# Inner norms: the summands of the tokens' tiles are added by adding transfers from memory, VectorE only multiplies

## The chip, the cores and the metric

The kernel runs on one core of one Trainium2 chip. The metric is the device time of one execution in microseconds; it is 1188.16 us before the change (median of 3 runs, 1187.76 to 1188.19). TensorE, VectorE, ScalarE, GpSimd and SyncE are called PE, DVE, ACT, POOL and SP, as in the profile.

## The reference, cut to what matters

Two layers, each of three post-norm steps on 256 tokens of width 1024, in float32:

```
for l in range(2):
    h = (silu(x @ w1) * (x @ w3)) @ w2            # width 2816
    x = LN(ALPHA * x + 0.5 * h) * g[l, 0] + b[l, 0]
    h = mixer(x)                                  # gated unit and differential attention
    x = LN(ALPHA * x + h) * g[l, 1] + b[l, 1]
    h = (silu(x @ w1') * (x @ w3')) @ w2'
    x = LN(ALPHA * x + 0.5 * h) * g[l, 2] + b[l, 2]
```

`g` and `b` are rows of 1024 numbers, the same for all tokens. The norm of the last step writes the output. The other five are the inner norms: their x is the input of the next step's products and also the term ALPHA * x of the next norm. The mixer's attention turns q and k by rotary angles: each pair of rows is multiplied by a cosine, the pair with its rows exchanged by a sine, and the two are added.

## The kernel before, in words

**Products.** The weights stream from memory once, in pieces of 128x2048 floats (1 MB), each fetched by SP into one of 4 buffers `raw`. ACT rounds a half of a piece to a high part (`whi`, L195 or L247), DVE subtracts it to get the low part (`wlo`, L197 or L249), and PE multiplies x, itself in a high and a low part, with both. The order of PE's instructions is written out by hand. On the other engines a scheduler sets the order when the kernel is built, by a priority that grows with every fetch, by expected times, and by some orders that the code asks for (`behind`, L158). It follows that an instruction taken away can move others on its engine. Within an engine the order is then fixed, and an instruction whose inputs are late holds all that follow it there. Results leave PE through 4 main banks of PSUM in rotation and 4 side banks.

**The inner norms** (class `Norm`). The tokens lie in two tiles `x_tok[0]` and `x_tok[1]` (`xtok` in the profile, 128 tokens by 1024 floats each). When a step ends, DVE adds the new term to these tiles (`part`, `fold`), takes mean and variance, and normalises them in place (`finish`). Then two things happen. The normalised tiles are turned to columns, scaled and shifted there by ACT (`affine`), and split for the next step's products: PE needs these at once. And the tiles themselves are multiplied by g and increased by b (`tokens`, L703), because the next norm, 100 us or more later, starts from them. For that, `bc_load` (L585) has POOL load g and b, each spread over 128 partitions, into two buffers with the tag `bc` (512 KB each); a one-column copy by DVE (L587) sets the earliest moment of the load. The two `bc` buffers also hold two tiles `planes` of the feed-forward step in turn, and the mixer's rows `gbias`, `g_bc` and `b_bc`.

**POOL's queue.** POOL issues the transfers that go through the software queue: the loads by `bc_load` and the adding transfers of `gather` (L353). These add 512 KB of weights from memory to a buffer in place, with `accum_op=ALU.add`; there are 22 of them before the change. Between them POOL copies the halves of 32-bit numbers apart and together for transposing transfers (L216, L229, L741), and multiplies in the mixer (L977).

**The mixer's first part.** After the columns of v, four pairs of calls of `rope` (L968), q and k of two heads each. A call streams 1 MB of weights through PE (16 matmuls of 512 columns with the high part and 16 of 256 with the low, 5.6 us), and its result comes out in two halves from two banks: ACT copies one part (`r`, L303), DVE adds the other (`z`, L305 or L307). Then SP issues two transfers that exchange neighbouring rows of z into `swap` (L973), DVE multiplies z by the cosine (L976), POOL multiplies `swap` by the sine (L977), and DVE adds both (L981). After each pair of calls `attend` (L987) follows in steps put beside later products: PE takes the scores (L1001), DVE and ACT the softmax (L1013, L1015), DVE the difference `d` of the two maps (L1024), POOL parts it for a transposing transfer of SP's queue (L216, L220), ACT joins it (L1049), and PE multiplies it with v (L1055, L1057).

In the list of functions, L numbers are those of the profile.

Of the kernel before, what the change touches and what calls it, by code (L numbers as in the profile page):

```python
# [17 lines left out]
ALU = mybir.AluOpType  # L18
AX = mybir.AxisListType

P = 128
# [33 lines left out]
def trunk(ctx, tc, x, xT, w13a, w13b, w2, wb, wqk, wu, wg, wgr, wbr, wbrr, wo, gateb, gatebr, sgug, sgub, sguwT, sgubias, lam, diffg,  # L55
          lng, lnb, lngT, lnbT, cosT, sinT, out):
    nc = tc.nc
    V, A, G, PE = nc.vector, nc.scalar, nc.gpsimd, nc.tensor
# [15 lines left out]
    def name(s):  # L74
        serial[0] += 1
        return f"{s}_{serial[0]}"
# [24 lines left out]
    def s512(s, n=4):  # L101
        return tmp.tile([P, 512], F32, tag="side", name=name(s), bufs=n)

    def sm(s, n, dtype=F32, bufs=2):
        return small.tile([P, n], dtype, tag=f"{s}{n}", name=name(s), bufs=bufs)
# [31 lines left out]
    def beside(task, delay):  # L137
        tasks.append([clock[0] + delay, task])
# [16 lines left out]
    def behind(ins):  # L155

        return tc.issue_after(ins) if ins is not None else nullcontext()
# [427 lines left out]
    def bc_load(src, after):  # L585
        t = res.tile([P, D], F32, tag="bc", name=name("bc"), bufs=2)
        V.tensor_copy(t[:, :1], after)  # L587
        spread[0] = G.dma_start(t, src.partition_broadcast(P)).ins
        return t

    class Norm:
# [6 lines left out]
        def __init__(self, l, i, scale, eps, after, last=False):  # L598
            self.scale, self.eps, self.last, self.done, self.front = scale, eps, last, set(), i
            self.ends, self.xhi, self.xlo, self.rows = [None] * NT, {}, {}, {}  # L600
            self.gT, self.bT = (v[:, l, i] for v in (ln_g, ln_b))
            self.y = x_tok
            self.group = 256 if last else 512
            self.st = [sm("st", D // self.group * 6, bufs=2) for _ in range(NT)]
            self.g, self.b = bc_load(lng[l, i], after), bc_load(lnb[l, i], after)
            if last:
                beside(self.halved(), 9)
                self.minus = s512("minus")
                A.activation(self.minus[:, :P], ident, AF.Copy, scale=-1.0)
                self.eps_t = self.minus[:, 2 * P : 2 * P + 1]  # L610
                V.memset(self.eps_t, eps)
                with behind(silu[0]):
                    A.activation(sm("first", 1), mask[:, :1], AF.Sqrt)
            else:
                self.via = []
                self.x = [xs.tile([P, 4, 512], F32R, tag="x", name=name("x")) for _ in range(2)]
# [85 lines left out]

        def tokens(self, t):  # L703
            with behind(added[0] if self.front else self.xlo[1, 1]):
                for v, op in ((self.g, ALU.mult), (self.b, ALU.add)):
                    V.tensor_tensor(out=self.y[t], in0=self.y[t], in1=v, op=op)
            yield 0

        def sent(self):
# [632 lines left out]
```

## Time and profile before

| what | value |
|---|---|
| time, median of 3 runs | 1188.16 us (1187.76 to 1188.19) |
| time of the profiled execution | 1187.27 us |
| its span in the profile | 1185.6 us, so 1.7 us lie around it |
| PE busy | 1180.0 us, 5775 matmuls |
| DVE busy | 1013.4 us (85%) |
| ACT, POOL busy | 826.7 us (70%), 281.7 us (24%) |
| PE clock granted | 1.0 throughout |
| bytes moved | 275.10 MB, 232 GB/s on average |

All times of single instructions are those of the one profiled execution, counted from the start of its span. An instruction that runs back to back with the next is shown with a little overlap (a DVE operation of 1.22 us is followed after 1.14). A row of the timeline has the start, the duration, engine, line, operation, output and inputs, and in brackets how long the engine stood idle before it and who ended that. A row of the windows has, after each engine's busy time, the granted clock, the share of the 16 DMA engines that was busy, and GB/s. The transfer groups show the median time from issue to landing.

### The profile page before, as it was taken

The numbers are of one execution on the slowest core, as the hardware profiler recorded it, in microseconds if no ns is written. First come the engines' busy times: TensorE is split into PE (matmuls) and PEld (weight loads), VectorE is DVE, ScalarE is ACT, GpSimd is POOL, SyncE is SP. The second block draws the span as 40 slices with busy tenths as digits, with TensorE's granted clock in tenths as the row PEclk, the third lists the DMA queues.
The fourth block names the chain that finished last, engine by engine and source line by source line (L and its number), as shares of the span: only waits on it lengthen the run. The fifth ranks groups of instructions, "written<-read, shape, count | busy, mean of one in ns | idle before, by whom it ended". The sixth has DMA issues, their size and how long they took to land.

```text
span 1185.6 us, 16672 instructions
## 1 busy us (share of the span) xinstructions
PE 1180.0 (100%) x5775; PEld 994.6 (84%) x5775; DVE 1013.4 (85%) x1560; ACT 826.7 (70%) x1417; POOL 281.7 (24%) x352
## 2 busy tenths in 40 slices
PE   9999999999999999999999999999999999999998
PEld 8888888888888888888888888888888888888887
DVE  7989989788688989889898889888965989988895
ACT  6688658559855677876667876676788556679761
POOL 1012201247420220061020141004564112102300
PEclk9999999999999999999999999999999999999999
DMA  9868976758865658689668689586666755786881
GB/s 358 262 199 260 289 274 210 263 191 239 245 211 169 224 194 271 188 272 272 232 223 264 194 278 271 200 300 224 216 203 203 257 182 165 260 247 210 272 253 36
DMA packets 129620, 275.10 MB, mean 232 GB/s; under 512 B 89040, under 2 KB 90368, under 8 KB 105472
## 3 DMA queue, kind: packets, MB, share of 16 engines
q1 hardware_dynamic: 121968, 248.67, 63.4%
q0 software_dynamic: 6992, 24.71, 8.9%
q8 instruction: 45, 0.74, 0.2%
q10 hardware_dynamic: 576, 0.66, 0.2%
q14 instruction: 39, 0.32, 0.1%
HBM read 248.05 MB, written 1.05 MB: 210 GB/s over the span
## 4 chain that ended last, share of the span: by engine, by line
PE 99%; DVE 0%; DVEq 0%; issue 0%
PE bank L283 46%; PE bank L295 15%; PE sbank L376 12%; PE bank L410 10%; PE bank L302 8%; PE sbank L410 3%; PE bank L527 2%; PE sbank L1001 1%; PE bank L376 1%; PE sbank L1057 1%; PE sbank L1175 1%; PE sbank L539 0%; PE sbank L1055 0%; PE sbank L698 0%; DVE xtok L685 0%; DVE xtok L679 0%
## 5 line engine op out<-in xcount | busy, mean ns | idle before, releaser
L197 DVE TENSOR_TENSOR wlo<-raw,whi 128x1024 fp32r<-128x1024 f32 (+1 forms) x346 | 378.3, 1121 | 53.0 <-ACT whi L195 39.7
L195 ACT ACTIVATE whi<-raw 128x1024 fp32r<-128x1024 f32 (+1 forms) x350 | 323.0, 951 | 131.7 <-PE bank L283 43.0
L283 PE MATMUL bank<-whi,x 128*128 128x512 f32 x1224 | 386.3, 390 | 0.0
L283 PEld LDWEIGHTS bank<-whi,x 128*128 128x128 f32 x1224 | 229.8, 188 | 47.6
L283 PE MATMUL bank<-wlo,x 128*128 128x512 f32 x612 | 238.2, 389 | 0.0
L249 DVE TENSOR_TENSOR wlo<-raw,whi 128x1024 fp32r<-128x1024 f32 (+1 forms) x123 | 143.8, 1193 | 21.4 <-ACT whi L247 12.5
L247 ACT ACTIVATE whi<-raw 128x1024 fp32r<-128x1024 f32 (+1 forms) x123 | 121.1, 1003 | 52.4 <-DVE raw L359 18.2
L295 PE MATMUL bank<-x,whi 128*128 128x512 f32 x640 | 153.3, 391 | 0.0
L295 PEld LDWEIGHTS bank<-x,whi 128*128 128x128 f32 x640 | 118.2, 188 | 23.8
L283 PEld LDWEIGHTS bank<-wlo,x 128*128 128x128 f32 x612 | 114.9, 188 | 23.4
L302 PEld LDWEIGHTS bank<-x,wlo 128*128 128x128 f32 x640 | 81.4, 191 | 2.9
L229 POOL COPY seven<-seven 128x512 uint16<-128x512 uint16 x16 | 49.4, 3130 | 140.4 <-ACT whi L195 54.6
L302 PE MATMUL bank<-x,wlo 128*128 128x256 f32 x640 | 82.6, 283 | 0.0
L410 PE MATMUL bank<-whi,hhi 128*128 128x512 f32 (+1 forms) x182 | 68.2, 374 | 0.0
L410 PE MATMUL bank<-whi,hlo 128*128 128x512 f32 (+1 forms) x182 | 67.9, 373 | 0.0
L410 PE MATMUL bank<-wlo,hhi 128*128 128x512 f32 (+1 forms) x182 | 67.9, 373 | 0.0
L977 POOL TENSOR_TENSOR swap<-swap,sin_t 128x512 f32<-128x512 f32 x16 | 27.8, 1735 | 101.8 <-DMA swap<-z 52.2
L741 POOL COPY nvia<-ntwo 128x256 uint16<-128x256 uint16 x20 | 9.9, 543 | 162.0 <-DMA ntwo<-nvia 142.5
L303 ACT ACTIVATE r<-bank 128x256 f32<-128x256 f32 x96 | 34.8, 372 | 16.7 <-PE bank L302 16.5
L376 PE MATMUL sbank<-whi,xhs 128*128 128x512 f32 x128 | 42.0, 389 | 0.0
L410 PEld LDWEIGHTS bank<-whi,hlo 128*128 128x128 f32 x182 | 34.3, 188 | 6.1
L410 PEld LDWEIGHTS bank<-wlo,hhi 128*128 128x128 f32 x182 | 34.3, 188 | 5.9
(285 smaller groups left out, 2158.7 us busy)
## 6 DMA issues: line engine op xcount, KB each, us to landing
raw<-in_w13b SPq DMA_DIRECT2D x68, 1024.0 KB, 6.1
raw<-in_w SPq DMA_DIRECT2D x32, 1024.0 KB, 7.0
raw<-in_wb SPq DMA_DIRECT2D x16, 1024.0 KB, 6.1
raw<-in_wqk SPq DMA_DIRECT2D x16, 1024.0 KB, 6.1
home<-in_w13b SPq DMA_DIRECT2D x16, 512.0 KB, 6.0
raw<-in_w13a SPq DMA_DIRECT2D x8, 1024.0 KB, 5.0
home<-in_w SPq DMA_DIRECT2D x16, 512.0 KB, 4.0
raw<-in_wgr SPq DMA_DIRECT2D x8, 1024.0 KB, 5.3
```

The costliest lines, as they stand in the source:

```text
L195: inline(A, A.activation(h, r, AF.Copy).ins)
L197: low = eng.tensor_tensor(out=w, in0=r, in1=h.bitcast(F32), op=ALU.subtract).ins
L229: eng.tensor_copy(out=o, in_=i)
L247: a = A.activation(hi, src, AF.Copy).ins
L249: return a, eng.tensor_tensor(out=lo, in0=src, in1=hi.bitcast(F32), op=ALU.subtract).ins
L283: PE.matmul(ps, xx, w, start=start and n == 0, stop=stop and n == 2)
L295: PE.matmul(b[-1], hi[:, k * P : (k + 1) * P], xc(k), start=k == 0, stop=False)
L302: PE.matmul(b[n][:, :T], lo[:, k * P : (k + 1) * P], xc(k)[:, :T], start=False, stop=k == KT - 1)
L303: emptied[0] = A.activation(r[:, s], b[n][:, T:], AF.Copy, scale=scale).ins
L376: PE.matmul(ps, x[o](k), y, start=start and k == n == 0, stop=stop and k == 3 and n == 2, skip_group_check=True)
L410: PE.matmul(q[c][t][:, :n] if o == 0 else more[:, :n], x(k, t), y, start=k == 8 and m == 0 and (c, t) != (1, 0), stop=k == FT - 1 and m == ...
L977: turned_by[0] = G.tensor_tensor(out=s3, in0=s3, in1=s, op=ALU.mult).ins
```

## The change

In the five inner norms `self.b` is no longer a tile that `bc_load` fills; it is the row in memory, seen as repeated over 128 partitions. `tokens` has DVE multiply by g as before, and then POOL issues a transfer that reads the row b for every partition and adds it to the token tile in place. The last norm still loads b.

```
-            self.g, self.b = bc_load(lng[l, i], after), bc_load(lnb[l, i], after)
+            self.g, self.b = bc_load(lng[l, i], after), lnb[l, i].partition_broadcast(P)
             if last:
+                self.b = bc_load(lnb[l, i], after)
                 beside(self.halved(), 9)
...
         def tokens(self, t):
             with behind(added[0] if self.front else self.xlo[1, 1]):
-                for v, op in ((self.g, ALU.mult), (self.b, ALU.add)):
-                    V.tensor_tensor(out=self.y[t], in0=self.y[t], in1=v, op=op)
+                V.tensor_tensor(out=self.y[t], in0=self.y[t], in1=self.g, op=ALU.mult)
+            G.dma_start(self.y[t], self.b, accum_op=ALU.add)
             yield 0
```

Ten DVE additions, five DVE copies of one column and five loads of b go; ten adding transfers of 512 KB come. Every line behind the first hunk is one higher in the changed file (L976 is L977, L981 is L982; the multiplication stays L706, since the loop's line goes, and the adding transfer is L707). PE's order is the same. On the other engines these places move; some rows of DVE and ACT in the feed-forward steps move as well, by one to four places.

DVE at the start of the first mixer's ropes, before: `z` is a rope's result, `bank` its two PSUM banks, `wlo` the low parts of weights, `swap` the exchanged rows.

```order
L307 SCALAR_TENSOR_TENSOR z_1965<-bank_1955,r_1964 128x256
L197 TENSOR_TENSOR wlo_2175<-raw_2168,whi_2174 128x1024
L976 TENSOR_TENSOR qk_1987<-z_1965,cos_t 128x512
L197 TENSOR_TENSOR wlo_2273<-raw_2270,whi_2272 128x1024
L305 TENSOR_TENSOR z_2023<-bank_2002,r_2022 128x256
L305 TENSOR_TENSOR z_2023<-bank_2011,r_2022 128x256
L197 TENSOR_TENSOR wlo_2277<-raw_2270,whi_2276 128x1024
L981 TENSOR_TENSOR qk_1987<-qk_1987,swap_1986 128x512
```

The same place on DVE in the changed kernel (the buffers have other numbers; L977 and L982 are L976 and L981 of before):

```order
L307 SCALAR_TENSOR_TENSOR z_1962<-bank_1952,r_1961 128x256
L197 TENSOR_TENSOR wlo_2172<-raw_2165,whi_2171 128x1024
L977 TENSOR_TENSOR qk_1984<-z_1962,cos_t 128x512
L197 TENSOR_TENSOR wlo_2270<-raw_2267,whi_2269 128x1024
L305 TENSOR_TENSOR z_2020<-bank_1999,r_2019 128x256
L982 TENSOR_TENSOR qk_1984<-qk_1984,swap_1983 128x512
L305 TENSOR_TENSOR z_2020<-bank_2008,r_2019 128x256
L197 TENSOR_TENSOR wlo_2274<-raw_2267,whi_2273 128x1024
```

The addition of the first rope's exchanged rows has moved ahead of the second half of the second rope's z. In the mixer of layer 1 the same two rows have changed places; in the later ropes of both mixers the order of before and of the change is the same, with L981 between the halves.

POOL at the norm ahead of the first mixer, before; `bc` is the tile of b, `nvia` the norm's turned halves, `x` the low parts that POOL makes:

```order
L588 DMA bc_1209<-in_lnb 128x1024
L353 DMA raw_1219<-in_w 128x1024 x2
L741 COPY nvia_1616<-ntwo_1757 128x256 x2
L249 TENSOR_TENSOR x_1213<-nvia_1616,x_1213 128x2x128 x2
L741 COPY nvia_1694<-ntwo_1800 128x256 x2
L977 TENSOR_TENSOR swap_1986<-swap_1986,sin_t 128x512
```

and in the changed kernel:

```order
L353 DMA raw_1216<-in_w 128x1024 x2
L742 COPY nvia_1613<-ntwo_1754 128x256 x2
L249 TENSOR_TENSOR x_1210<-nvia_1613,x_1210 128x2x128 x2
L742 COPY nvia_1691<-ntwo_1797 128x256 x2
L707 DMA xtok_143<-in_lnb 128x1024
L707 DMA xtok_144<-in_lnb 128x1024
L978 TENSOR_TENSOR swap_1983<-swap_1983,sin_t 128x512
```

The load of b is gone from its place behind that of g, and two adding transfers stand directly ahead of POOL's first multiplication by the sine.

POOL after a norm that leads to a feed-forward step, in the changed kernel; `planes` are the first gated products being parted for their transposes:

```order
L742 COPY nvia_4273<-ntwo_4399 128x256 x2
L216 COPY planes_4448<-planes_4448 128x512 x2
L707 DMA xtok_143<-in_lnb 128x1024
L216 COPY planes_4516<-planes_4516 128x512 x2
L707 DMA xtok_144<-in_lnb 128x1024
L353 DMA raw_4565<-in_w13b 128x1024 x2
```

Before, the same rows stood there without the two transfers. On SP, in two of the three steps (those of the second feed-forward), the transposing transfer of the second `planes` now stands ahead of two loads of 512 KB (`home`) that it followed.

## The prediction

> **What bounds the kernel now.** I read the page from the top: the engines' busy time, the chain that ended last, and then PE's groups, shapes apart, for idle time.
>
> ```profile
> span 1185.6 us, 16672 instructions
> PE 1180.0 (100%) x5775; PEld 994.6 (84%) x5775; DVE 1013.4 (85%) x1560; ACT 826.7 (70%) x1417; POOL 281.7 (24%) x352
> PE 99%; DVE 0%; DVEq 0%; issue 0%
> L283 PE MATMUL bank<-whi,x 128*128 128x512 f32 x1224 | 386.3, 390 | 0.0
> L539 PE MATMUL sbank<-warm 128*128 128x128 bf16 x37 | 4.1, 313 | 1.0 <-DVE warm L535 1.0
> L677 PE MATMUL sbank<-bc,minus 128*128 128x256 f32 x6 | 1.6, 396 | 0.7 <-ACT minus L675 0.7
> ```
>
> PE is the chain from end to end. The groups of matmuls show idle time in front of two only, 1.0 us ahead of the warm-up and 0.7 us in the last norm, and the change touches neither. So nothing that becomes cheaper on another engine can shorten the run by more than a fraction of a microsecond: **a gain is excluded almost by construction**, and the question is whether something now comes too late for PE.
>
> **What is removed.** Ten additions on DVE, five loads of b, five one-column copies.
>
> ```profile
> L706 DVE TENSOR_TENSOR xtok<-xtok,bc 128x1024 f32<-128x1024 f32 x20 | 26.7, 1340 | 0.0
> ```
>
> The group holds the multiplications and the additions, 20 in 26.7 us; ten of them are 13.4 us of DVE's 1013.4. On the path they are worth 0, because PE waited for nothing in these stages: DVE does them behind the last split of x that PE needs, and what it does next comes earlier without PE being able to use it. The token tiles are wanted again by the next norm only, 100 us later, so the landing of the sum is not urgent either. What is late next after this "gain" is PE itself, as before.
>
> **What is added: ten adding transfers.** Before has 22 transfers of this kind and size (8 + 8 + 6), with weights as source. Their price in the 16 DMA engines' time follows from the two queues.
>
> ```profile
> q1 hardware_dynamic: 121968, 248.67, 63.4%
> q0 software_dynamic: 6992, 24.71, 8.9%
> home<-in_w POOLq DMA_DIRECT2D x8, 512.0 KB, 8.7
> raw<-in_w POOLq DMA_DIRECT2D x8, 512.0 KB, 7.4
> raw<-in_w13b POOLq DMA_DIRECT2D x6, 512.0 KB, 8.4
> ```
>
> SP's queue q1 moved 248.67 MB in 63.4% of 1185.6 us, 3.02 us per MB. POOL's queue q0 took 8.9%, 105.5 us, for 24.71 MB. Of these, 22 x 0.524 = 11.53 MB were additions; the other 13.18 MB at q1's price are 39.8 us, so the additions took 65.7 us, **2.99 us of all 16 engines each**. A plain 512 KB at q1's price is 1.59 us. That is the lower bound for the new transfers, whose source is one row read 128 times like that of the loads of b; I take 2.99, the row of the same operation, and 4.0 as upper bound, a third more. (The Trainium skill, "DMA: Bandwidth & Descriptors", section "Anatomy of one DMA — SWDGE (gpsimd) path", fits such a transfer as 2.0 us fixed plus bytes over 436 GB/s, an estimate of 1.2 us of moving for 512 KB; the queues' rows here speak against that for additions.)
>
> **Where they collide: the ropes of the mixers.** In both mixers POOL issues its two additions right after the multiplications, from about 197 us on in layer 0. What do the DMA engines do then?
>
> ```profile
> 195.00:200.00 5.00, 5.00 (x23) 4.13 (x22) 5.00 (x8) 4.97 (x8) 0.00 (x0) 1.00 0.96 352
> 200.00:205.00 5.00, 5.00 (x24) 4.14 (x23) 5.00 (x6) 4.74 (x6) 0.00 (x0) 1.00 0.69 236
> 205.00:210.00 5.00, 5.00 (x31) 4.47 (x30) 5.00 (x6) 2.22 (x5) 0.00 (x0) 1.00 0.94 349
> 210.00:215.00 5.00, 5.00 (x32) 4.43 (x31) 3.34 (x6) 2.41 (x4) 0.00 (x0) 1.00 1.00 382
> ```
>
> The column before the last is the DMA share. From 195 to 215 it leaves (0.04 + 0.31 + 0.06 + 0.00) x 5 = 2.05 us free; the two additions need 5.98. If the engines serve both queues and waste nothing, whatever stands at the end of SP's queue around 215 comes **3.9 us later**. At that end stands the first exchange of rows, `swap`:
>
> ```profile
> 209.07 1.17 SPq L973 DMA_DIRECT2D swap<-z  x2
> 215.56 1.30 POOL L977 TENSOR_TENSOR swap<-swap,sin_t 128x512 f32<-128x512 f32 x1 [25.01 <-DVE wlo L197]
> 213.59 0.75 DVE L305 TENSOR_TENSOR z<-bank,r 128x256 f32<-128x256 f32 x2
> 216.89 0.69 DVE L981 TENSOR_TENSOR qk<-qk,swap 128x512 f32<-128x512 f32 x1 [1.43 <-POOL swap L977]
> 217.50 0.68 DVE L976 TENSOR_TENSOR qk<-z,cos_t 128x512 f32<-128x512 f32 x1
> 214.36 1.10 SPq L973 DMA_DIRECT2D swap<-z  x2
> 218.62 1.86 POOL L977 TENSOR_TENSOR swap<-swap,sin_t 128x512 f32<-128x512 f32 x1 [1.76 <-DMA swap<-z]
> 221.61 1.11 SPq L973 DMA_DIRECT2D swap<-z  x2
> 224.35 1.60 POOL L977 TENSOR_TENSOR swap<-swap,sin_t 128x512 f32<-128x512 f32 x1 [3.87 <-DMA swap<-z]
> ```
>
> The first exchange takes 6.5 us from issue to POOL's start, the third, on freer queues, 2.74. Before, this did not matter: both halves of the second z (L305, twice) were out at 214.34, SP issued the second exchange at 214.36, and only then DVE waited for POOL (L981 at 216.89, POOL done at 216.86). **The change puts L981 between the two halves.** The second half now waits for the first exchange: with nothing else changed it starts where L976 did, at 217.50, lasts 0.42, and the second exchange goes out at 217.94 instead of 214.36. It finds freer queues and takes 2.74 instead of 4.26, so POOL starts at 220.68 instead of 218.62: 2.1 us late by the order alone, 2.1 + 3.9 = 6.0 with the queue.
>
> **Is there slack?** From here the rows follow each other without a gap: POOL done, L981, second half of z, next exchange, POOL, three times over. The far end of it is the joining of `d` by ACT for PE:
>
> ```profile
> 241.69 2.16 POOL L216 COPY aT<-d 128x512 uint16<-128x512 uint16 x2
> 243.88 1.23 SPq L220 DMA_TRANSPOSE d<-aT  x1
> 245.20 1.18 SPq L973 DMA_DIRECT2D swap<-z  x2
> 247.96 1.29 POOL L977 TENSOR_TENSOR swap<-swap,sin_t 128x512 f32<-128x512 f32 x1 [4.11 <-DMA swap<-z]
> 258.37 0.80 ACT L1049 ACTIVATE d<-d 128x256 uint16<-128x256 uint16 x2
> 259.56 0.38 PE L1055 MATMUL sbank<-val,d 128*128 128x128 f32 x2
> ```
>
> POOL's copies end at 243.85, the transposing transfer is issued at 243.88, SP's next exchange at 245.20 (the transpose holds SP for 1.23), POOL is at it from 247.96 to 249.25, then DVE takes L981 and the second softmax with ACT, and behind that ACT joins `d`, done at 259.17. PE uses it at 259.56. **The slack is 0.39 us.** None of these steps waits for PE, so a lateness goes through: PE stands 6.0 - 0.4 = 5.6 us in the mixer of layer 0 (1.7 by the order alone). The half z late in its bank, from which PE would want to go on at about 220.6 (estimate: the middle of the 16 matmuls from 218.71), is no cost on top, since the same lateness is counted once.
>
> In layer 1 the same place has more air:
>
> ```profile
> 800.25 1.30 POOL L977 TENSOR_TENSOR swap<-swap,sin_t 128x512 f32<-128x512 f32 x1 [22.83 <-DMA swap<-z]
> 803.45 1.54 POOL L977 TENSOR_TENSOR swap<-swap,sin_t 128x512 f32<-128x512 f32 x1 [1.91 <-DMA swap<-z]
> 806.32 0.68 DVE L981 TENSOR_TENSOR qk<-qk,swap 128x512 f32<-128x512 f32 x1
> 842.55 0.80 ACT L1049 ACTIVATE d<-d 128x256 uint16<-128x256 uint16 x2
> 845.96 0.38 PE L1055 MATMUL sbank<-val,d 128*128 128x128 f32 x2
> 785.00:790.00 5.00, 5.00 (x23) 4.13 (x22) 5.00 (x6) 4.48 (x6) 0.00 (x0) 1.00 0.89 323
> 790.00:795.00 5.00, 5.00 (x31) 4.45 (x30) 4.96 (x6) 2.97 (x5) 0.00 (x0) 1.00 0.70 249
> ```
>
> POOL is done with the first exchange at 801.55; L981 and the half of z then take about 1.0, the next exchange 2.74, POOL 1.54, so the second L981 comes at 806.9 instead of 806.32, 0.6 late. With the queue's lateness (free until 800: 0.55 + 1.5 us, the same 2.05) it is 4.5. The slack at the end is 845.96 - 843.35 = 2.6, so PE stands 1.9.
>
> **The feed-forward steps** cost 0. Six additions fall there, one behind each multiplication; POOL issues them after the copies that something waits for. The cover is free time of the DMA engines and early loads:
>
> ```profile
> 435.00:440.00 5.00, 5.00 (x24) 4.14 (x23) 5.00 (x6) 4.31 (x5) 0.48 (x1) 1.00 0.68 218
> 440.00:445.00 5.00, 5.00 (x24) 4.14 (x23) 5.00 (x5) 0.63 (x1) 2.56 (x2) 1.00 0.55 185
> ```
>
> Here 3.85 us are free for the first addition's 2.99. If the cover were gone, each could cost up to its 2.99 us, 18 in all; PE's weights are split several microseconds ahead there, so I count none of it. SP's transpose ahead of `home` makes those loads about 3 us later, with the same cover.
>
> **Sum.** 5.6 + 1.9 = 7.5 us. Against the profiled execution's 1187.27 (span 1185.6 and 1.7 around it) that is 1194.8; it lies 0.9 under the median of the runs, so for a median I forecast 1188.16 + 7.5 = **1195.7 us**.
>
> **Rivals.**
> *The queue has room (not slower).* The additions start 11 us before the first exchange is issued, and the rows of their kind land after 7.4 to 8.7 us. Should they be through by then without holding the 1 MB loads, only the order counts: 1.7 us in layer 0, 0 in layer 1, 1189.9; and if a slow link of the chain (POOL's 1.29 to 1.86 for one multiplication, for instance) is shorter this time, 1188.2. It decides at a lateness of the first exchange of 0.7 us, since 1.7 + 0.7 is 0.2%. Against it: a share of 0.94 and 1.00 just there. By the Trainium skill's fit (same page and section) the pair would need 2.4 us, hold the exchange by 0.35, and give 1190.2, inside this case.
> *The addition is dearer or hits the weights.* At 4.0 us each the lateness is 6.0: 7.7 + 4.0 = 11.7, 1199.9; if loads of the feed-forward steps come late as well, up to 18 more.
> *Nothing changes,* because the chain regains the time before PE needs it: 1188.2. For it speaks that DVE has 13.4 us less to do; against it that the chain's rows show DVE waiting for POOL, not the reverse.
> *Faster:* no row gives it; 1187, if the 0.39 us and its like were stalls in other executions.
>
> **How the numbers follow.** Chances: the late chain by order and queue 0.55 (1191 to 1200), room in the queue 0.17 (1188.2 to 1190.2), nothing 0.12, dearer 0.13 (1200 and more), faster 0.03. 0.2% is 2.4 us, about what a measurement of this kernel can tell from no change. So slower by more than that 0.55 + 0.13 = 0.68, within it 0.17 + 0.12 = 0.29, faster 0.03. The range from 1188.0 to 1201.0 leaves out the dear case's upper part and the faster one.
>
> **What would show it.** In the changed profile: DVE's L982 of the first rope about 4 us later than 216.89, with POOL as its releaser; SP's second exchange at 222 instead of 214.4; PE idle ahead of L1056 or at the ropes' banks, some 5 to 6 us in layer 0 and about 2 in layer 1; the DMA share near 1.0 from 195 to 215; no idle PE elsewhere. If the first exchange lands as before, the queue's part is wrong; if it lands late and PE does not stand, the slack is. If PE waits for `whi` or `wlo` after a norm, I placed the cost wrongly.

## The result, and the profile after

The change makes the kernel slower by a little: 1190.36 us (median of 16 runs, 1188.96 to 1194.94) against 1187.42 us (1186.74 to 1189.91) for the kernel before on the same chip, a ratio of 1.0028 with a 95% interval from 1.0021 to 1.0035. The medians are 2.9 us apart, and the interval is 2.5 to 4.2 us; forecast were 7.5. The profiled execution took 1190.81 us.

The page of the changed kernel, the lines that answer to those of before:

```profile
span 1189.1 us, 16681 instructions
PE 1181.2 (99%) x5775; PEld 994.0 (84%) x5775; DVE 999.3 (84%) x1545; ACT 824.8 (69%) x1417; POOL 292.9 (25%) x357
...
PE 95%; DVE 2%; DMA 1%; issue 1%; ACT 0%; POOL 0%; SPq 0%; DVEq 0%; POOLq 0%; ACTq 0%
...
raw<-in_wqk SPq DMA_DIRECT2D x16, 1024.0 KB, 8.6
home<-in_w13b SPq DMA_DIRECT2D x16, 512.0 KB, 12.5
```

DVE has 14.1 us less to do and the kernel is slower. The chain that ended last, before almost PE alone, now runs through DVE and DMA as well: PE stands somewhere. The loads of `wqk`, the weights of the ropes, land after 8.6 us (6.1 before), those of `home` after 12.5 (6.0). To find where PE stands, I compared the start of each of its instructions with that of the same instruction before. The difference grows in three places: by 1.4 us at L1056 in the mixer of layer 0 (and 0.3 more at 275 us), by 0.3 at 466 to 472 us, and by 0.9 at 641 to 644 us, both in feed-forward steps. The two profiled spans differ by 3.5 us: 2.9 stand ahead of PE's last product, the other 0.6 behind it.

One correction is needed for what follows. A profile counts from the start of its own span, and the first 7 us of the spans differ: after them PE is up to 0.3 us earlier (the run without additions, 0.26) or 0.5 later (three later runs) than in the profile of before, and stays so until its first stall. Where instants of two kernels are compared below "on PE's clock", this difference is taken off.

The first place in the timeline, from the first exchange of rows to the product that waits:

```profile
213.58 0.42 DVE L305 TENSOR_TENSOR z<-bank,r 128x256 f32<-128x256 f32 x1
216.31 1.29 POOL L978 TENSOR_TENSOR swap<-swap,sin_t 128x512 f32<-128x512 f32 x1 [17.21 <-ACT whi L195]
217.63 0.69 DVE L982 TENSOR_TENSOR qk<-qk,swap 128x512 f32<-128x512 f32 x1 [3.63 <-POOL swap L978]
218.24 0.42 DVE L305 TENSOR_TENSOR z<-bank,r 128x256 f32<-128x256 f32 x1
218.69 1.11 SPq L974 DMA_DIRECT2D swap<-z  x2
221.38 1.31 POOL L978 TENSOR_TENSOR swap<-swap,sin_t 128x512 f32<-128x512 f32 x1 [3.78 <-DMA swap<-z]
...
260.02 0.79 ACT L1050 ACTIVATE d<-d 128x256 uint16<-128x256 uint16 x2
260.91 0.46 PE L1056 MATMUL sbank<-val,d 128*128 128x128 f32 x2 [1.20 <-issue]
```

The mechanism is the one forecast: L982 stands between the two halves of z, DVE waits 3.63 us there, the second exchange goes out at 218.69 instead of 214.36, and PE stands ahead of L1056. But the first exchange is late by 0.75 us only (216.31 against 215.56; PE's clocks agree to 0.01 here), where 3.9 were forecast. The windows of the same stretch:

```profile
195.00:200.00 5.00, 5.00 (x24) 4.13 (x23) 5.00 (x8) 4.97 (x8) 1.74 (x2) 1.00 1.00 367
200.00:205.00 5.00, 5.00 (x24) 4.14 (x23) 5.00 (x5) 4.73 (x6) 0.00 (x0) 1.00 1.03 254
205.00:210.00 5.00, 5.00 (x31) 4.47 (x30) 3.17 (x6) 1.83 (x4) 0.00 (x0) 1.00 1.03 347
210.00:215.00 5.00, 5.00 (x32) 4.43 (x31) 2.06 (x3) 2.78 (x4) 0.00 (x0) 1.00 1.01 417
215.00:220.00 5.00, 5.00 (x31) 4.47 (x30) 2.37 (x4) 2.89 (x4) 1.29 (x1) 1.00 0.42 173
```

The DMA share (the column before the last) is 1.0 from 195 to 215, as said; but in the last window before 215 the engines moved 417 GB/s, where before they moved 382 at a share of 1.00. And from 215 on there is room again.

The second kind of place, in the feed-forward steps. After a norm SP issues a transposing transfer of `planes` at 445.51 us, and POOL an addition at 445.43. All that SP's queue holds behind the two comes late. First the group of `home` before (issues from 441 to 460 us), then the groups of the changed kernel (444 to 460 us):

```profile
home<-in_w13b SPq DMA_DIRECT2D x4, 512.0 KB, 5.8
```
```profile
home<-in_w13b SPq DMA_DIRECT2D x4, 512.0 KB, 15.5
xtok<-in_lnb POOLq DMA_DIRECT2D x1, 512.0 KB, 15.0
planes<-planes SPq DMA_TRANSPOSE x1, 15.4
```

The same happens to the pair at 623.75 and 623.84 us (14.2 and 14.5 us to landing). There DVE waits for `home`, and PE for DVE's split, in the next layer's first step:

```profile
639.56 1.23 DVE L359 TENSOR_TENSOR raw<-raw,home 128x1024 f32<-128x1024 f32 x1 [4.64 <-DMA home<-in_w13b]
643.71 0.50 PE L376 MATMUL sbank<-wlo,xhs 128*128 128x512 f32 x1 [0.54 <-DVE wlo L249]
```

### The profile page after: what moved, and what is told of

It reads as the page before. It is cut to its first block, busy times and chain, and to the rows that moved or that the text cites. A ratio compares the mean times of both kernels' runs of the same rounds, so it can differ in the third digit from the quotient of the medians.

```text
span 1189.1 us, 16681 instructions
## 1 busy us (share of the span) xinstructions
PE 1181.2 (99%) x5775; PEld 994.0 (84%) x5775; DVE 999.3 (84%) x1545; ACT 824.8 (69%) x1417; POOL 292.9 (25%) x357
## 4 chain that ended last, share of the span: by engine, by line
PE 95%; DVE 2%; DMA 1%; issue 1%; ACT 0%; POOL 0%; SPq 0%; DVEq 0%; POOLq 0%; ACTq 0%
PE bank L283 42%; PE bank L295 15%; PE sbank L376 11%; PE bank L410 9%; PE bank L302 8%; PE sbank L410 3%; PE bank L527 2%; DMA home<-in_w13b 1%; PE sbank L1002 1%; PE bank L376 1%; PE sbank L1058 1%; PE sbank L1176 1%; DVE wlo L197 0%; PE sbank L539 0%; PE sbank L1056 0%
## 5 line engine op out<-in xcount | busy, mean ns | idle before, releaser
L283 PEld LDWEIGHTS bank<-whi,x 128*128 128x128 f32 x1224 | 229.8, 188 | 47.8
L295 PE MATMUL bank<-x,whi 128*128 128x512 f32 x640 | 153.3, 391 | 0.0
L295 PEld LDWEIGHTS bank<-x,whi 128*128 128x128 f32 x640 | 118.2, 188 | 23.8
L229 POOL COPY seven<-seven 128x512 uint16<-128x512 uint16 x16 | 57.4, 3641 | 124.7 <-ACT whi L195 45.7
L359 DVE TENSOR_TENSOR raw<-raw,home 128x1024 f32<-128x1024 f32 x32 | 39.1, 1234 | 9.8 <-DMA home<-in_w13b 9.8
L978 POOL TENSOR_TENSOR swap<-swap,sin_t 128x512 f32<-128x512 f32 x16 | 24.6, 1540 | 90.7 <-DMA swap<-z 44.0
L1016 ACT ACTIVATE pp<-pp,mx 128x256 f32<-128x256 f32 (+1 forms) x64 | 28.2, 443 | 21.2 <-DVE mx L1014 21.2
## 6 DMA issues: line engine op xcount, KB each, us to landing
home<-in_w13b SPq DMA_DIRECT2D x16, 512.0 KB, 12.5
```

The source lines that it names most:

```text
L229: eng.tensor_copy(out=o, in_=i)
L283: PE.matmul(ps, xx, w, start=start and n == 0, stop=stop and n == 2)
L295: PE.matmul(b[-1], hi[:, k * P : (k + 1) * P], xc(k), start=k == 0, stop=False)
L359: inline(V, V.tensor_tensor(out=v, in0=v, in1=m, op=ALU.add).ins)
```

## The experiments

All ratios are against runs of the kernel before on the same chip; 0.1% is 1.2 us. Three theories at the start. **Theory 1:** the order of DVE in the first ropes costs about 1.6 us in the mixer of layer 0, and the additions that meet transposing transfers cost about 1.2 us in the feed-forward steps; the exchange is hardly late because DVE, relieved of the additions, frees the buffers of the loads sooner. **Theory 2:** all of it is the load of the transfers on the DMA engines. **Theory 3:** all of it is DVE's order.

### The order without the transfers

```
-            G.dma_start(self.y[t], self.b, accum_op=ALU.add)
```

> The changed kernel with its ten adding transfers left out (b is therefore not added in the inner norms); every engine keeps the order of the changed kernel, VectorE's too. Theory 1 (the order of VectorE in the first ropes costs about 1.6 us in the mixer of layer 0, the transfers about 1.2 us in the feed-forward steps): PE still stands about 1.4 us ahead of L1055 in layer 0, the second exchange still goes out about 3 us later than 214.36, nothing is lost in the feed-forward steps; time over before +1.0 to +1.8 us, ratio about 1.0012. Theory 2 (all of the loss is the transfers' load on the DMA engines, in the mixers as well): no loss, ratio 1.000 or a little below. Theory 3 (all of the loss is the order, and the feed-forward steps' part is chance): +2.5 to +3.

Measured: 1186.88 us, ratio 0.9997 (0.9988 to 1.0006). No loss, and no stall in the profile. In the timeline DVE's order is that of the changed kernel:

```profile
213.23 1.32 POOL L977 TENSOR_TENSOR swap<-swap,sin_t 128x512 f32<-128x512 f32 x1 [23.00 <-DMA swap<-z]
214.59 0.69 DVE L981 TENSOR_TENSOR qk<-qk,swap 128x512 f32<-128x512 f32 x1 [0.85 <-POOL swap L977]
215.20 0.42 DVE L305 TENSOR_TENSOR z<-bank,r 128x256 f32<-128x256 f32 x1
215.64 1.10 SPq L973 DMA_DIRECT2D swap<-z  x2
259.30 0.38 PE L1055 MATMUL sbank<-val,d 128*128 128x128 f32 x2
```

The first exchange is 2.33 us earlier than before, **2.1 on PE's clock**. From there to the second exchange it takes 2.41 us, as forecast for the new order (2.38), so that the lead is used up by it and nothing is late at PE. Why is it earlier? The loads of `wqk` go out sooner, at 200.21, 202.48 and 204.81 instead of 201.59, 205.00 and 207.27 (1.1 to 2.3 us on PE's clock), since DVE reaches their predecessors' splits sooner without its two additions. Theory 3 falls, and Theory 1 as it was put: the order costs nothing as long as the exchange leads. And the transfers do have a price here: with them the exchange comes 3.08 us later (216.31 against 213.23), 2.8 on PE's clock, where 3.9 were forecast. The lateness of 0.75 is thus the difference of two terms, 2.8 for the transfers and 2.1 for the relief of DVE.

### The order undone, with the transfers

```
-        def rope(src, scale):
+        def rope(src, scale, apart=1.55):
...
-            beside(rest(), 1.55)
+            beside(rest(), apart)
...
-            qT = rope(wqk[l, hp, 0], HD ** -0.5)
+            qT = rope(wqk[l, hp, 0], HD ** -0.5, 1.55 if hp else 1.9)
```

> The changed kernel, with the first rope's addition started 1.9 instead of 1.55 beats behind it, so that VectorE does both halves of the second rope's z ahead of L982, as before the change; the ten adding transfers stay. Theory 1: second exchange back at about 214.4, no stall ahead of L1055 in layer 0 (or one below 0.8 us, from the 0.75 us by which the first exchange lands late), the feed-forward steps' loss stays; +0.8 to +1.6 us over before, ratio about 1.001. Theory 2: as the changed kernel, +2.9, since the transfers are unchanged. Theory 3: 0.

Measured: 1189.87 us, ratio 1.0022 (1.0013 to 1.0031): as slow as the changed kernel. PE stands 1.4 us ahead of L1056, although the second exchange goes out at 214.25:

```profile
216.40 1.30 POOL L978 TENSOR_TENSOR swap<-swap,sin_t 128x512 f32<-128x512 f32 x1 [17.38 <-DMA swap<-z]
217.73 0.69 DVE L982 TENSOR_TENSOR qk<-qk,swap 128x512 f32<-128x512 f32 x1 [3.51 <-POOL swap L978]
218.94 3.46 DVE L197 TENSOR_TENSOR wlo<-raw,whi 128x1024 fp32r<-128x1024 f32 x2
222.32 0.41 DVE L307 SCALAR_TENSOR_TENSOR z<-bank,r 128x256 f32<-128x256 f32 x1
```

This edit did not bring the whole order back. Before, DVE did a split `wlo` (1.22 us) while it waited for the exchange; here, as in the changed kernel, that split stands behind L982 and helps to push the third rope's z (L307) to 222.32, against 219.24 before. On PE's clock that is 3.2 us: 0.95 by which L982 itself is late, 1.1 for the split, and 1.1 because the second of the two splits lasts 2.32 us instead of 1.22. What holds it is open. It is not the half of z alone that counts, but all that DVE could do in the wait and now does after it. My expectation missed that.

### DVE filled up again, with the transfers

```
+            if not last and (not i):
+                self.spare = res.tile([P, D], F32, tag="bc", name=name("bc"), bufs=2)
             if last:
...
                 V.tensor_tensor(out=self.y[t], in0=self.y[t], in1=self.g, op=ALU.mult)
+                if not self.front:
+                    V.tensor_tensor(out=self.spare, in0=self.g, in1=self.g, op=ALU.add)
```

> The changed kernel with an addition of equal size on VectorE (g + g into a spare tile) behind each multiplication ahead of the mixers, so that VectorE has as much to do there as before and its order in the ropes is that of before; the ten adding transfers stay. Theory 1 with its explanation of the small queue term (VectorE, relieved, frees the buffers of the loads sooner, so the loads go out sooner): now the relief is gone, the loads in 200 to 208 us are issued at their old times, and the first exchange reaches POOL 2.5 to 4 us later than 215.56; L982 is that much late and VectorE behind it; PE stands 1 to 3 us ahead of L1055 in layer 0; with the feed-forward steps' part +2 to +4. Rival (the additions simply fit into the queue): first exchange at most 1 us late, no stall in the mixers, +0.8 to +1.6.

Measured: 1188.01 us, ratio 1.0009 (1.0000 to 1.0018), with DVE's order that of before, split included. PE starts the product of L1055 at 259.55 (259.56 before). With the full load on DVE **and** the transfers the exchange is late by 0.5 us only (0.6 on PE's clock), so the rival named here is right and my explanation of the small term wrong in this form. Theory 2 falls too, since the transfers are all there and PE loses 0.4 us in this mixer, no more:

```profile
213.47 0.74 DVE L305 TENSOR_TENSOR z<-bank,r 128x256 f32<-128x256 f32 x2
214.13 1.21 DVE L197 TENSOR_TENSOR wlo<-raw,whi 128x1024 fp32r<-128x1024 f32 x1
216.07 1.29 POOL L982 TENSOR_TENSOR swap<-swap,sin_t 128x512 f32<-128x512 f32 x1 [15.70 <-DMA swap<-z]
```

Where did the transfers' time go? The two queues from 195 to 220 us (packets, MB, share of the 16 engines), first of the kernel before, then of this one:

```profile
q1 hardware_dynamic: 1336, 7.91, 87.5%
```
```profile
q1 hardware_dynamic: 1323, 7.82, 79.9%
q0 software_dynamic: 288, 1.05, 21.2%
```

The pair of additions took 21.2% of 25 us, 5.3 us, **2.65 us each** (2.99 were forecast). SP's queue moved about the same bytes in less time: 21.9 us for 7.91 MB, 2.77 us per MB, before; 20.0 us for 7.82 MB, 2.55 per MB, here. So room for the 5.3 us came from the free 12.5% (3.1 us) and from quicker packets (0.22 x 7.8 = 1.7 us), 4.8 in all; the missing 0.5 is about the lateness seen. That is arithmetic on one execution of each, and the quicker packets are not shown to be an effect of the additions: the run with the change ahead of the feed-forward steps only (below), whose mixers are those of before, took 2.70 us per MB here, moved 413 GB/s at a share of 1.02 from 210 to 215 us, and had the exchange 1.1 us earlier than before. What does follow is that a share of 1.00 with 382 GB/s was not a full engine.

The first exchange at POOL in the four combinations, on PE's clock, with the other runs that belong there:

| | DVE as loaded as before | DVE relieved |
|---|---|---|
| no additions here | 215.56 (kernel before), 214.45 (feed-forward only) | 213.50 (no additions), 213.51 (mixers' later), 213.63 (all moved) |
| with additions | 216.19 (DVE refilled) | 216.32 (changed kernel), 216.51 (order undone), 216.88 (L982 behind), 217.09 (mixers only) |

With the additions the exchange comes at 216.2 to 217.1, whether the loads go out early or late; without them it comes earlier the earlier the loads are issued. The two values at the upper left have the same loads at the same times, so a lateness taken from one profile of each can be wrong by about 1 us.

### The change ahead of the mixers only

```
-            self.g, self.b = bc_load(lng[l, i], after), lnb[l, i].partition_broadcast(P)
+            self.g, self.adds = bc_load(lng[l, i], after), not last and (i == 0)
+            self.b = lnb[l, i].partition_broadcast(P) if self.adds else bc_load(lnb[l, i], after)
...
-                V.tensor_tensor(out=self.y[t], in0=self.y[t], in1=self.g, op=ALU.mult)
-            G.dma_start(self.y[t], self.b, accum_op=ALU.add)
+                for v, op in ((self.g, ALU.mult), (self.b, ALU.add))[: 1 if self.adds else 2]:
+                    V.tensor_tensor(out=self.y[t], in0=self.y[t], in1=v, op=op)
+            if self.adds:
+                G.dma_start(self.y[t], self.b, accum_op=ALU.add)
```

> The change made only for the norms ahead of the mixers (four adding transfers); the norms ahead of the feed-forward steps as before, with the loads of b and the additions on VectorE. Theory 1: mixer of layer 0 as in the changed kernel (about 1.4 to 1.7 us ahead of L1055), feed-forward steps as before, with the loads of home landing about 6 us after their issue; +1.2 to +1.9. Theory 2 (load on the DMA engines): four tenths of the loss, +1.1, spread over the stages. Theory 3: +2.5 to +3.

Measured: 1189.87 us, ratio 1.0025 (1.0016 to 1.0034), in the profile all but 0.2 us of it in the mixer of layer 0. In this execution the exchange reached POOL at 216.89, and PE stood 2.31 us ahead of the same product, against 1.20 in the changed kernel's:

```profile
262.12 0.46 PE L1058 MATMUL sbank<-val,d 128*128 128x128 f32 x2 [2.31 <-issue]
```

The four runs make a new form of the theory. **Theory 1b:** the additions make the first exchange late, by 0.6 to 1.5 us against the profile of before; that becomes a stall of PE because the new order leaves 1.5 us of DVE's work (half a z and a split) behind the waiting L982. Either alone costs little or nothing; the loss in the feed-forward steps is an occasional one.

### L982 placed behind the work that need not wait

```
-        def rope(src, scale):
+        def rope(src, scale, steps=0):
...
+                tc.cur_priority += steps * STEP
                 with behind(added[0]):
                     V.tensor_tensor(out=r, in0=r, in1=sw, op=ALU.add)
+                tc.cur_priority -= steps * STEP
...
-            qT = rope(wqk[l, hp, 0], HD ** -0.5)
+            qT = rope(wqk[l, hp, 0], HD ** -0.5, 0 if hp else 4)
```

> The changed kernel with L982 of the first rope given a later place in VectorE's queue: ahead of it stand both halves of the second rope's z, the split `wlo` and the cosine product L977, so that VectorE works while it would wait for the exchange. All ten adding transfers stay. Theory 1b (the loss is the lateness of the first exchange by the transfers, made into a stall of PE by the 1.5 us of VectorE's work that the new order leaves behind the waiting L982): the first exchange still reaches POOL about 0.8 us later than before, 216.3, the second goes out at about 214.3, the scaled z (L307) of the third rope at 219.2 to 220 as before; PE stands 0 to 0.6 us ahead of L1055 in layer 0; time +0.2 to +0.9 us over before. Rival (the second exchange or the loads themselves, held by the transfers, are what is late): as the changed kernel, +2.5 to +3.

Measured: 1188.20 us, ratio 1.0009 (1.0000 to 1.0017), just over the range expected. Two thirds of the loss are gone with DVE's order alone, though the exchange is later here than in the changed kernel:

```profile
214.35 1.10 SPq L974 DMA_DIRECT2D swap<-z  x2
216.87 1.30 POOL L978 TENSOR_TENSOR swap<-swap,sin_t 128x512 f32<-128x512 f32 x1 [17.77 <-DMA swap<-z]
219.95 0.42 DVE L307 SCALAR_TENSOR_TENSOR z<-bank,r 128x256 f32<-128x256 f32 x1
259.92 0.46 PE L1058 MATMUL sbank<-val,d 128*128 128x128 f32 x2 [0.20 <-issue]
```

The lateness of 1.3 at the exchange is 0.7 at L307 (219.24 before) and 0.36 at PE, the forecast slack of 0.39 taken off.

### The change ahead of the feed-forward steps only

The same edit as for the mixers, with `i > 0` in place of `i == 0`.

> The change made only for the norms ahead of the feed-forward steps (six adding transfers); ahead of the mixers as before. Theory 1b (the loss sits in the mixer of layer 0, and the stalls of 0.3 and 0.9 us that one profile showed in the feed-forward steps are rare): 0 to +0.8 us. Theory 1 in its first form: +1.2. Rival (the loss goes by the number of transfers): six tenths, +1.7.

Measured: 1187.79 us, ratio 1.0005 (0.9996 to 1.0014); no stall in its profile. So the mixers' part is 2.7 us, and this one 0.6, with 1.7 as the interval's end. The first exchange in this profile, in a mixer that is that of before (0.53 have to be taken off for PE's clock):

```profile
214.98 2.17 POOL L980 TENSOR_TENSOR swap<-swap,sin_t 128x512 f32<-128x512 f32 x1 [23.94 <-DVE z L305]
```

### The mixers' additions 95 us later

```
+            if not self.front:
+                yield 34
+                with behind(added[0]):
+                    V.tensor_copy(self.y[t][:, :1], self.y[t][:, :1])
             G.dma_start(self.y[t], self.b, accum_op=ALU.add)
```

> The changed kernel with the four additions ahead of the mixers issued 34 beats, some 95 us, later, behind a one-column copy on VectorE that makes them wait, where no exchange of the ropes is under way; order of VectorE as in the changed kernel otherwise. Theory 1b: the first exchange as in the run without additions, POOL at 213.2; no stall ahead of L1055; -0.3 to +0.6 us. Rival (the load of the transfers costs wherever it falls): +1.7 to +3.

Measured: 1187.91 us, ratio 1.0004 (0.9995 to 1.0013), the exchange at 213.97 (213.51 on PE's clock, as in the run without additions), no stall. The median is 0.75 us above that of before, where 0.6 was the most expected, but the interval holds no difference: the same bytes, elsewhere, cost nothing that can be told.

### Written instead of added

```
-            G.dma_start(self.y[t], self.b, accum_op=ALU.add)
+            G.dma_start(self.y[t], self.b)
```

> The changed kernel with the ten transfers at the same places, of the same size and source, but writing b over the token tile instead of adding it (the norms' result is lost, b stands in its place). It measures what of the price is the addition. If an addition is dearer than a plain write (2.7 us of the 16 engines for one by the changed kernel's rows, 1.6 by the price of the other queue): the pair takes 3.2 us of the engines in 195 to 220 instead of 5.3, the loads of wqk land about 2 us later than without transfers instead of 5, the first exchange reaches POOL at 214 to 215, and PE stands 0 to 0.7 us; time -0.2 to +0.8. Rival (a transfer on POOL's queue costs the same either way): as the changed kernel, +2.5 to +3.

Measured: 1188.22 us, ratio 1.0009 (1.0000 to 1.0018). The queue's row from 195 to 220 us, and the exchange:

```profile
q0 software_dynamic: 288, 1.05, 12.4%
```
```profile
214.98 1.29 POOL L978 TENSOR_TENSOR swap<-swap,sin_t 128x512 f32<-128x512 f32 x1 [15.72 <-DMA swap<-z]
```

A plain write of 512 KB takes 12.4% of 25 us by two, **1.55 us** of the 16 engines, the addition 2.65: the difference is the addition's own. By the fit in the Trainium skill, "DMA: Bandwidth & Descriptors", section "Anatomy of one DMA — SWDGE (gpsimd) path", moving 512 KB takes 1.2 us, an estimate; the plain write's 1.55 is nearer to it than the addition's 2.65. The exchange comes 1.0 us later than without transfers (on PE's clock), with the additions 2.8 to 3.6. The profile shows PE losing 0.3 us in the mixer of layer 0; the median is 1.1 us above that of before, a little over the range expected. Beside the transposing transfers of the feed-forward steps all six plain writes land after 4.6 to 5.9 us; of the additions issued at these places in seven profiles, 17 of 42 took more than 10 us.

### Twice the additions ahead of the mixers

```
             G.dma_start(self.y[t], self.b, accum_op=ALU.add)
+            if not self.front:
+                G.dma_start(self.y[t], self.b, accum_op=ALU.add)
```

> The changed kernel with each of the four additions ahead of the mixers issued twice (b is added twice there); the second pair waits for the first to land. Same order on every engine otherwise. If in the changed kernel the 16 engines have no room left from 200 us to the first exchange (theory 1b: with the additions it reaches POOL at 216.1 to 216.9 whether the loads go out early or late), what the second pair moves ahead of the exchange, 2.7 to 5.3 us of the engines, comes on top in full: first exchange at POOL at 219 to 222, PE stands 4 to 7 us ahead of L1055 in layer 0, and in layer 1, where the slack was used up to 0.9, it stands another 1 to 4; +5 to +11 over before. Rival (there is still room, since a share of 1.0 did not mean full before the change either): first exchange below 218, +3 to +4.5.

Measured: 1201.07 us, ratio 1.0115 (1.0101 to 1.0129), which is 13.8 us over before where at most 11 were expected. The exchange comes at 222.20, 5.9 us behind that of the changed kernel, where two additions take 5.3, so the second pair is paid in full: after the first, nothing is free. PE now stands much earlier, where the second half of z holds a bank (L295), and its clock falls:

```profile
222.20 1.26 POOL L980 TENSOR_TENSOR swap<-swap,sin_t 128x512 f32<-128x512 f32 x1 [9.07 <-DMA swap<-z]
224.57 3.78 PE L295 MATMUL bank<-x,whi 128*128 128x512 f32 x8 [3.89 <-DVE z L305]
```
```profile
220.00:222.00 2.00, 0.68 (x3) 0.22 (x2) 0.00 (x0) 0.00 (x0) 0.00 (x0) 1.00 0.99 401
222.00:224.00 2.00, 0.00 (x0) 0.00 (x0) 0.51 (x1) 0.00 (x0) 1.26 (x1) 0.74 0.18 74
224.00:226.00 2.00, 1.43 (x3) 1.16 (x4) 2.00 (x4) 1.60 (x3) 0.00 (x0) 0.50 0.16 61
226.00:228.00 2.00, 2.00 (x6) 1.60 (x5) 1.72 (x3) 0.00 (x0) 0.72 (x1) 0.50 0.72 168
```

PE would have started this product at 220.7, 0.1 from the 220.6 estimated in the prediction. At 224.6 it is 4.0 us behind the kernel before, at 229.8 it is 6.5, since the granted clock is 0.50 from 224 to 228. The same happens in layer 1 after a stall of 2.68 us. My expectation had no term for the clock.

### Everything moved out of the way

The two edits of L982 and of the mixers' additions together, and the additions of the feed-forward steps 7 and 5 beats later in the same manner.

> The version that the runs point to: the change with the additions ahead of the mixers issued 34 beats later, those ahead of the feed-forward steps 7 and 5 beats later (all behind a one-column copy on VectorE that makes them wait), and L982 behind the split and the cosine product in VectorE's queue. Theory 1b: nothing is late any more, and PE, the bound, gains nothing: -0.5 to +0.5 us over before, the loads of home landing at about 6 us. Rival (the six or ten one-column copies, the transfers' load or a new order cost something): +1 to +2.

Measured: 1188.13 us, ratio 1.0008 (0.9999 to 1.0017), with no stall in the profile (span 1185.5 us; 1185.6 before). The best form of the change is no gain: PE is the bound. The median stays 0.9 us above that of before, more than expected. About half of that lies outside the span: the runs' times exceed their spans by 2.1 us here and by 1.7 before (medians). Why is not settled, and the interval reaches to no difference. The loads of `home` land after 8.3 us, so it did not bring them back to 6.

## Why the prediction was right or wrong

**The bound, and no gain.** Right. The work taken off DVE (14.1 us in the changed kernel) bought nothing in any run; the fastest version, without the additions, is at 0.9997.

**Where it goes wrong.** Right in the place and the chain: L982 between the halves of z, the second exchange late, the join of `d` by ACT at the end of it, PE ahead of L1056 with a slack of 0.39. By the order alone POOL was to start on the second exchange at 220.68; with the 0.75 of the first one's lateness taken off it was 220.63. Not all of the lateness goes through as said: POOL's multiplications shortened when they came later (1.31 for 1.86, 1.27 for 1.60), and 2.8 us at the second exchange are 1.65 at ACT. One path was not seen: the split that the change also leaves behind L982. With the second exchange back at 214.25 PE stood as long, since DVE came late to the third rope's z.

**The step that failed: "whatever stands at the end of SP's queue around 215 comes 3.9 us later."** The price in it was nearly right (2.65 us an addition for 2.99), and the effect against a kernel that lacks the additions alone is 2.8 us on PE's clock. Two things were left out. The removed additions freed DVE just ahead of that stretch, which sends the loads and with them the exchange 2.1 us ahead; I had priced that relief at 0 because PE could not use it, and did not ask which transfers it would start. And the free time of the engines was taken to be 1 minus the share, while SP's queue also got through with 2.55 us of the engines per MB with additions beside it, after 2.77 before; how much of that is chance is open, since a profile with the mixers of before had 2.70. With additions and the new order the exchange is late by 0.8 to 1.5 us against the profile of before, not 3.9, and PE in layer 0 loses 1.7 to 3.1, not 5.6. The figure of the rival "the queue has room", 1.7 us for the order alone, came out nearly right by luck, since its reason is not the one: without additions the same order costs nothing.

**Layer 1: 1.9 forecast, 0 measured.** The first exchange came at 805.60, on PE's clock (2.91 us late by then) 2.4 late for the 3.9 forecast, and the second L982 at 812.03, 2.8 late for 4.5. ACT's join of `d` was 1.7 late, and at the end a slack was left:

```profile
847.18 0.81 ACT L1050 ACTIVATE d<-d 128x256 uint16<-128x256 uint16 x2
848.86 0.38 PE L1056 MATMUL sbank<-val,d 128*128 128x128 f32 x2
```

ACT is done at 847.99, 0.87 ahead of PE.

**The feed-forward steps: 0 forecast, 1.2 in the changed kernel's profile, none of 0.15 us or more in six other profiles with the same additions.** The cover, splits several microseconds ahead, holds in most executions. What the forecast lacked is that an addition beside a transposing transfer can hold the queue for 15 us, not 3. What makes the slowest executions (up to 1194.94) is open. That it is these six additions is not borne out: with them alone none of 11 executions took more than 1188.30, while the change ahead of the mixers only has one of 1193.97.

## What to carry over

An engine that is not the bound still sends transfers and fills waits: when work is taken off it, ask which loads go out sooner, and which of its instructions now stand behind one that waits. The order alone cost nothing here and the lateness alone 0.4 us of PE's time; together they cost 1.7 to 3.1 in the profiles, and putting the one waiting instruction behind work that need not wait gave most of it back. A DMA share near 1.0 doesn't tell how much more the engines can take; compare the time per MB, and move a transfer with no hurry out of the stretch where urgent ones run.

## What the runs showed of the hardware

An adding transfer of 512 KB took 2.65 us of the 16 DMA engines (21.2% of 25 us for two), a plain one through the same queue 1.55 (12.4%).

Additions and transposing transfers in flight together can both be slow: the addition took 10 to 17 us to land in 17 of 42 cases, and the transfer beside it about as long, where six plain writes at these places took 4.6 to 5.9. The changed kernel, and beside it the one with plain writes, in the same window (DMA share and GB/s at the end):

```profile
440.00:445.00 5.00, 5.00 (x23) 4.13 (x23) 5.00 (x7) 1.83 (x3) 2.08 (x2) 1.00 1.41 48
```
```profile
440.00:445.00 5.00, 5.00 (x24) 4.14 (x23) 5.00 (x6) 1.59 (x2) 2.94 (x3) 1.00 0.80 208
```

A share of 1.41 with 48 GB/s: the packets are in the engines and hardly move. It happens in some executions and places and not in others that look alike; what decides it is open.

In the run with twice the additions PE stood for 3.89 us, from 220.7 on, and then ran at a granted clock of 0.50 for some 5 us, which cost 2.5 us more. The mean clock of 0.74 from 222 to 224 puts the fall at about 223, 2.3 us after PE stopped. In the same run, in layer 1, a stall of 2.68 us was enough:

```profile
817.39 3.44 PE L295 MATMUL bank<-x,whi 128*128 128x512 f32 x8 [2.68 <-DVE z L305]
...
818.00:820.00 2.00, 2.00 (x6) 1.61 (x5) 2.00 (x3) 0.69 (x1) 0.00 (x0) 0.50 0.65 180
```

The stall of 2.31 us in the run with the mixers only left it at 1.00. The Trainium skill, "TensorE: Matmul & The Clock Gate", section "Part 1: The HAM clock gate", says that the clock halves after an idle window of about 3.4 us that runs freely. That it halves is what the trace shows; it did so here in a stall of 2.68 us already, so the figure is no safe bound for this kernel. A stall of 2.7 us or more cost more than itself here.
